# Stick-breaking attention on one Trainium2 core: high parts taken straight from PSUM, weights kept in PSUM for their low part, q stacked by DMA, last key block 128 wide

## The chip, the cores and the metric

The kernel runs on one core of one Trainium2 chip. The metric is the device time of one execution in microseconds (us); smaller is better. The engines are called as the profile calls them: PE (matmul), DVE (VectorE), ACT (ScalarE), POOL (GpSimd) and SP (SyncE, which here only issues DMAs).

## What is computed

The reference is a two-layer trunk over 512 positions of width 1024: an RG-LRU layer, a SwiGLU feed-forward layer (FFN), a stick-breaking attention layer with 16 heads of width 64, and a second FFN, each with an RMSNorm ahead of it and a residual add behind. The change touches the attention alone, whose core is, for each head (cut from the reference):

```python
z = jnp.einsum("bhqd,bhkd->bhqk", qb, k32) * scale
mask = key_pos[None, :] < q_pos[:, None]
log_beta = jax.nn.log_sigmoid(z)
log_1m = jnp.where(mask, jax.nn.log_sigmoid(-z), 0.0)
suffix = lax.cumsum(log_1m, axis=3, reverse=True) - log_1m
wts = jnp.where(mask, jnp.exp(log_beta + suffix), 0.0)
return jnp.einsum("bhqk,bhkd->bhqd", wts, v32)
```

All of it is to be exact to nearly float32.

## The kernel before, in words

**Two parts for every operand.** TensorE multiplies in float32r, a rounded float32. The kernel therefore splits each operand into a high part (a copy into a float32r tile, which rounds) and a low part (the operand minus the high part) and adds the products high by high, high by low and low by high in PSUM. Most of the work of DVE, ACT and POOL is such splitting: weights arrive by DMA as 128x1024 chunks `raw`, ACT copies the high part `wh` (L236) and DVE or POOL subtracts the low part `wl` (L237).

**Attention, per head.** Scores are held transposed, keys on the partitions and queries along the free axis, in four key blocks of 128 keys. Key block `kt` only meets queries from its own block on, so its tile is `ZW[kt]` = 512, 384, 256, 256 queries wide; the last one holds 128 columns more than it needs, which are masked. A head has three PSUM banks: one for block 0, one for block 1, and one for blocks 2 and 3 side by side. Two sets of three banks alternate between even and odd heads, so head h+2 reuses the banks of head h; the last two banks serve the projections and the output. The steps are:

- `proj(t, part)` (PE, L270 to L272): one 128-row tile of q (t even) or k (t odd) for a pair of heads, 24 matmuls of 512 columns in two halves of 12, called P0 and P1 here. `proj_evac1` (DVE, L854) scales it into `tt`. `proj_evac2` splits it: for q into `qh` and `ql` of each head, 64 rows that are written twice, into both halves of the partitions (ACT L863 and L867, DVE L868 and L869), for k into `ks` of each head, high part in one half of the partitions, low part in the other (ACT L874, DVE L875).
- `s1(h)` (PE, L888 to L894): scores of head h, four blocks, each with `qh`, `ql` and a bf16 mask matmul.
- `chain_a(h)`: for each of three banks ACT does Abs, Exp and Ln (L910 to L912), DVE adds max(z, 0) in a `scalar_tensor_tensor` that reads the bank (L913, into `sp`), DVE casts the high part `sph` (L914) and POOL subtracts the low part `spl` (L915). For the third bank DVE also adds its two halves, casts the high part `r` and POOL subtracts the low part (L919 to L921).
- `s2(h)` (PE, L940): 16 matmuls add the suffix sums onto the scores in the same banks.
- `chain_b(h)`: for each bank ACT takes Exp from PSUM into an SBUF tile `t` (L955), DVE casts the high part `awh` (L956); then the low part `awl` is subtracted (L961), on DVE for the second bank (and the third from head 12 on), on POOL for the others.
- `s3(h)` (PE, L970): 8 matmuls, weights times `v`; then ACT copies half of the result (L978) and DVE adds it to the other half into `o` (L979). `osplit` (ACT L996, DVE L997) later splits a pair's `o` for the output projection `out_part`.

**What sets the order.** The loop over h from 0 to 16 is written out under a manual schedule: PE, ACT, DVE and POOL execute in the order of the code, each on its own, and wait on semaphores for one another. The body of iteration h is: P0 of tile t = h+3, `s1(h+1)`, `chain_a(h+1)` of the first two banks, P1 and `proj_evac1`, `chain_a(h+1)` of the third bank, `s3(h-1)`, `proj_evac2(t)`, perhaps an `osplit`, `s2(h)`, `chain_b(h)`. The split of the weights of the next tile is put ahead of `chain_a` on its engines. Only SP's order is left to the scheduler. An iteration with t odd is called a k iteration here (h even), one with t even a q iteration. Tiles of 128x512 come from a ring of reused slots (`new`, `rel`), temporaries from a ring of six (`tmp`); whoever writes a reused slot waits for its last readers.

Of the kernel before, what the change touches and what calls it, by code (L numbers as in the profile page):

```python
# [97 lines left out]
class Kern:  # L98
# [682 lines left out]
    def attention(self):  # L781
        nc, tc = self.nc, self.tc
        mm = nc.tensor.matmul
        ZW = (512, 384, 256, 256)
        QO = (0, 128, 256, 256)
        with ExitStack() as cx:
# [10 lines left out]
            msk = ap_.tile([P, 2 * P], BF16, name="msk")  # L797
# [7 lines left out]
            nc.gpsimd.affine_select(out=msk[:, P:2 * P], in_=msk[:, P:2 * P], compare_op=ALU.is_ge, fill=0.0,  # L805
# [50 lines left out]
            def proj_evac2(t):  # L856
                p, isk = divmod(t, 2)
                tt = self.tt
                lo, hi = slice(0, 64), slice(64, 128)
                if not isk:  # L860
                    for j, (own, oth) in enumerate(((lo, hi), (hi, lo))):
                        qh, ql = self.new("qh", F32R), self.new("ql", F32R)
                        nc.scalar.copy(qh[own], tt[own])  # L863
# [4 lines left out]
                        nc.vector.tensor_tensor(ql[own], tt[own], qh[own].bitcast(F32), ALU.subtract)  # L868
                        nc.vector.tensor_copy(ql[oth], ql[own].bitcast(F32))  # L869
                        heads[2 * p + j] = dict(qh=qh, ql=ql)  # L870
                else:
                    for j, (own, oth) in enumerate(((lo, hi), (hi, lo))):
                        ks = self.new("ks", F32R)
                        nc.scalar.copy(ks[own], tt[own])  # L874
                        nc.vector.tensor_tensor(ks[oth], tt[own], ks[own].bitcast(F32), ALU.subtract)  # L875
                        heads[2 * p + j]["ks"] = ks

            def zslot(h):
                b = zb[3 * (h % 2):3 * (h % 2) + 3]
                return (b[0][:, 0:512], b[1][:, 0:384], b[2][:, 0:256], b[2][:, 256:512]), b  # L880

            def s1(h):
                hd = heads[h]
                zt, b = zslot(h)
                for kt in range(4):
                    qs = slice(QO[kt], S)
                    lk = hd["ks"][:, ts(kt)]
                    mm(zt[kt], lhsT=lk, rhs=hd["qh"][:, qs], start=kt < 3, stop=False, skip_group_check=True)  # L888
                    mm(zt[kt], lhsT=lk, rhs=hd["ql"][:, qs], start=False, stop=False, skip_group_check=True)
                    if kt < 3:  # L890
                        mm(zt[kt][:, 0:P], lhsT=idb, rhs=msk[:, P:2 * P], start=False, stop=True,
                           skip_group_check=True)
                    else:
                        mm(zt[kt], lhsT=idb, rhs=msk, start=False, stop=True, skip_group_check=True)  # L894
                self.rel(hd["qh"], hd["ql"], hd["ks"])

            BW = (512, 384, 512)

            def chain_a(h, banks=(0, 1, 2)):
# [4 lines left out]
                for i in banks:  # L904
                    w = BW[i]
                    e, sp = self.tmp(), self.tmp()
                    sh = sph[i] = self.new("sph", F32R)
                    sl = spl[i] = self.new("spl", F32R)
                    z = b[i][:, :w]
                    nc.scalar.activation(e[:, :w], z, AF.Abs)  # L910
                    nc.scalar.activation(e[:, :w], e[:, :w], AF.Exp, scale=-1.0)
                    nc.scalar.activation(e[:, :w], e[:, :w], AF.Ln, bias=1.0)  # L912
                    nc.vector.scalar_tensor_tensor(sp[:, :w], z, 0.0, e[:, :w], ALU.max, ALU.add)  # L913
                    nc.vector.tensor_copy(sh[:, :w], sp[:, :w])  # L914
                    nc.gpsimd.tensor_tensor(sl[:, :w], sp[:, :w], sh[:, :w].bitcast(F32), ALU.subtract)  # L915
                    if i == 2:
# [28 lines left out]
            def chain_b(h):  # L945
# [3 lines left out]
                ts_ = []  # L949
                for i in range(3):  # L950
                    w = BW[i]
                    t = self.tmp()
                    ts_.append(t)
# [1 line left out]
                    nc.scalar.activation(t[:, :w], b[i][:, :w], AF.Exp)  # L955
                    nc.vector.tensor_copy(wh[:, :w], t[:, :w])  # L956
                for i in range(3):
                    w = BW[i]
# [1 line left out]
                    eng = nc.vector if i == 1 or (i == 2 and h >= 12) else nc.gpsimd  # L960
                    eng.tensor_tensor(wl[:, :w], ts_[i][:, :w], hd["wh"][i][:, :w].bitcast(F32), ALU.subtract)  # L961
# [188 lines left out]
```

## Time and profile before

| what | value |
|---|---|
| runs of the kernel | 1194.64 us median of 3 (1192.91 to 1197.56) |
| the profiled execution | 1194.11 us, its span 1192.4 us |
| PE busy over the span | 1139.0 us (96%) |
| DVE busy over the span | 884.0 us (74%) |
| ACT busy over the span | 647.1 us (54%) |
| POOL busy over the span | 356.8 us (30%) |
| the head loop's s1 and s2, first to last | about 572 to 787 us of the span |

A time inside the profile is counted from the start of the span. Busy time counts an instruction from start to end; two matmuls overlap at their ends, so the distance from start to start is what one costs in a row of them. A row of a timeline gives start, length, engine, line, operation, output and inputs, shape and count; in a table of groups the count is followed by total busy time, mean length in ns, and the idle time of the engine just before, with whoever ended it.

### The profile page before, as it was taken

What the parts mean: (1) busy time and instruction counts of PE and PEld (TensorE: products, weight loads), DVE (VectorE), ACT (ScalarE), POOL (GpSimd) and SP (SyncE); (2) the same over time, 40 slices, a digit from 0 to 9 for tenths busy, and PEclk for the clock granted to TensorE, in tenths of its full rate; (3) what the DMA queues carried; (4) which work ended last, traced back from release to release, by engine and by line L of the source; (5) the groups of instructions that cost most, each with busy time, mean ns of one, the idle gap of its engine ahead of it and who ended that gap; (6) DMA issues with size and microseconds to landing.
All of it is one profiled execution on the core that took longest, in us unless ns stands there. A gap on an engine that the chain in (4) does not pass through costs nothing.

```text
span 1192.4 us, 14205 instructions
## 1 busy us (share of the span) xinstructions
PE 1139.0 (96%) x5363; PEld 939.9 (79%) x5363; DVE 884.0 (74%) x1117; ACT 647.1 (54%) x935; POOL 356.8 (30%) x214
## 2 busy tenths in 40 slices
PE   9999999999999999999989888899999999999995
PEld 6887787888888888888767767678788888888884
DVE  7878889675757656544899999978967666675655
ACT  6698576534343434434677777757553434353431
POOL 2451223111111021451466665632311120211231
PEclk9999999999999999999999999899999999999997
DMA  7222344332323222322111111123422232322201
GB/s 235 85 88 88 107 139 144 106 105 73 121 74 115 80 88 73 104 89 71 53 36 53 37 36 36 36 70 126 154 92 93 84 107 88 124 88 89 71 18 71
DMA packets 30741, 105.83 MB, mean 89 GB/s; under 512 B 3536, under 2 KB 4560, under 8 KB 30672
## 3 DMA queue, kind: packets, MB, share of 16 engines
q1 hardware_dynamic: 30384, 104.40, 26.1%
q8 instruction: 42, 0.69, 0.2%
q10 hardware_dynamic: 288, 0.52, 0.1%
q14 instruction: 27, 0.22, 0.1%
HBM read 102.81 MB, written 2.10 MB: 88 GB/s over the span
## 4 chain that ended last, share of the span: by engine, by line
PE 63%; DVE 20%; ACT 4%; issue 4%; DMA 1%; POOL 1%; DVEq 0%; ACTq 0%; POOLq 0%
PE bank L631 10%; PE bank L632 10%; PE bank L633 10%; PE bank L654 7%; PE bank L652 7%; PE bank L653 7%; DVE wl L237 4%; PE bank L270 3%; PE bank L271 3%; PE bank L272 3%; DVE sph L914 3%; DVE t L913 2%; PE bank L638 1%; DVE r L920 1%; ACT wh L236 1%
## 5 line engine op out<-in xcount | busy, mean ns | idle before, releaser
L237 POOL TENSOR_TENSOR wl<-raw,wh 128x1024 fp32r<-128x1024 f32 (+1 forms) x74 | 178.8, 2416 | 619.6 <-ACT wh L236 619.6
L236 ACT CAST wh<-raw 128x1024 fp32r<-128x1024 f32 (+1 forms) x154 | 156.0, 1016 | 186.4 <-PE bank L633 88.4
L631 PE MATMUL bank<-wh,ow 128*128 128x512 f32 (+1 forms) x480 | 180.2, 375 | 3.8 <-DVE st L389 3.8
L632 PE MATMUL bank<-wl,ow 128*128 128x512 f32 (+1 forms) x480 | 178.9, 373 | 0.0
L633 PE MATMUL bank<-wh,ow 128*128 128x512 f32 (+1 forms) x480 | 178.8, 373 | 0.0
L237 DVE TENSOR_TENSOR wl<-raw,wh 128x1024 fp32r<-128x1024 f32 (+1 forms) x80 | 104.4, 1308 | 45.4 <-ACT wh L236 44.4
L236 ACT CAST wh<-tt 128x1024 fp32r<-128x1024 f32 x66 | 69.4, 1052 | 111.0 <-PE bank L653 55.1
L652 PE MATMUL bank<-hh,wh 128*128 128x512 f32 (+1 forms) x324 | 125.4, 387 | 0.0
L653 PE MATMUL bank<-hl,wh 128*128 128x512 f32 (+1 forms) x324 | 125.3, 387 | 0.0
L654 PE MATMUL bank<-hh,wl 128*128 128x512 f32 (+1 forms) x324 | 125.3, 387 | 0.0
L657 DVE TENSOR_TENSOR x<-x,bank 128x512 f32<-128x512 f32 x87 | 59.6, 685 | 85.2 <-PE bank L654 84.3
L270 PE MATMUL bank<-uh,wh 128*128 128x512 f32 x256 | 105.1, 410 | 4.4 <-DVE t L854 4.1
L237 DVE TENSOR_TENSOR wl<-tt,wh 128x1024 fp32r<-128x1024 f32 x66 | 80.7, 1223 | 36.4 <-ACT wh L236 36.0
L631 PEld LDWEIGHTS bank<-wh,ow 128*128 128x128 f32 x480 | 90.8, 189 | 20.0 <-issue 2.6
L633 PEld LDWEIGHTS bank<-wh,ow 128*128 128x128 f32 x480 | 90.8, 189 | 15.9
L632 PEld LDWEIGHTS bank<-wl,ow 128*128 128x128 f32 x480 | 90.9, 189 | 15.3
L272 PE MATMUL bank<-uh,wl 128*128 128x512 f32 x256 | 101.5, 397 | 1.0 <-DVE wl L237 1.0
L271 PE MATMUL bank<-ul,wh 128*128 128x512 f32 x256 | 102.1, 399 | 0.0
L237 DVE TENSOR_TENSOR wl<-b,wh 128x1024 fp32r<-128x1024 f32 x44 | 54.9, 1247 | 51.7 <-ACT wh L236 51.5
L236 ACT CAST wh<-b 128x1024 fp32r<-128x1024 f32 x44 | 46.3, 1053 | 62.1 <-PE bank L633 26.7
L915 POOL TENSOR_TENSOR spl<-t,sph 128x512 fp32r<-128x512 f32 (+1 forms) x48 | 58.9, 1233 | 58.3 <-DVE sph L914 47.9
L654 PEld LDWEIGHTS bank<-hh,wl 128*128 128x128 f32 x324 | 60.9, 188 | 12.4
(222 smaller groups left out, 2554.6 us busy)
## 6 DMA issues: line engine op xcount, KB each, us to landing
raw<-w_gu SPq DMA_DIRECT2D x44, 512.0 KB, 3.5
b<-w_gu SPq DMA_DIRECT2D x44, 512.0 KB, 4.2
raw<-w_dn SPq DMA_DIRECT2D x44, 512.0 KB, 3.5
raw<-w_qk SPq DMA_DIRECT2D x16, 512.0 KB, 3.5
raw<-w_in SPq DMA_DIRECT2D x14, 512.0 KB, 4.0
raw<-w_ao SPq DMA_DIRECT2D x8, 512.0 KB, 3.6
raw<-w_v SPq DMA_DIRECT2D x8, 512.0 KB, 3.4
raw<-w_bo SPq DMA_DIRECT2D x8, 512.0 KB, 3.5
```

The source lines that it names most:

```text
L236: self.nc.scalar.copy(wh[:, c], raw[:, c])
L237: self.wl_engine(i).tensor_tensor(wl[:, c], raw[:, c], wh[:, c].bitcast(F32), ALU.subtract)
L270: mm(out, lhsT=wh, rhs=xh, start=first, stop=False)
L271: mm(out, lhsT=wh, rhs=xl, start=False, stop=False)
L272: mm(out, lhsT=wl, rhs=xh, start=False, stop=last)
L631: mm(out[j][:, :w], lhsT=oh[:, ts(j)], rhs=wh[:, ws], start=st, stop=False, skip_group_check=True)
L632: mm(out[j][:, :w], lhsT=oh[:, ts(j)], rhs=wl[:, ws], start=False, stop=False, skip_group_check=True)
L633: mm(out[j][:, :w], lhsT=ol[:, ts(j)], rhs=wh[:, ws], start=False, stop=en, skip_group_check=True)
L652: mm(out, lhsT=w[0][:, ws], rhs=h[:, cs], start=st, stop=False, skip_group_check=True)
L653: mm(out, lhsT=w[0][:, ws], rhs=lw[:, cs], start=False, stop=False, skip_group_check=True)
L654: mm(out, lhsT=w[1][:, ws], rhs=h[:, cs], start=False, stop=en, skip_group_check=True)
L657: nc.vector.tensor_tensor(self.x[m], self.x[m], bank, ALU.add)
```

## The change

The attention function is edited in six places; everything else of the kernel is the same.

1. The last key block becomes 128 queries wide (`ZW`, `QO`). Its scores lie in columns 128 to 256 of the third bank (`ZO`), next to block 2 in 256 to 512, so the third bank's ACT and DVE work is 384 wide instead of 512. Its `sp` is one fixed tile `sp2` whose first 128 columns are zeroed once, so that the two halves can still be added. The mask is 128 wide everywhere.
2. `chain_a`: `sph` is no longer a cast of `sp` but a second `scalar_tensor_tensor` that reads the bank again and rounds on its output.
3. The low part of `r` is subtracted by DVE instead of POOL.
4. `chain_b`: ACT takes Exp twice, once from the bank into `awh` (which rounds), once in place in the bank; DVE then subtracts `awh` from the bank into `awl`, for all three banks. The three casts, and POOL's and DVE's subtractions from SBUF, are gone.
5. q: one ACT copy and one DVE subtraction of the whole 128x512 tile make `xh` and `xl` of the pair; eight DMAs of 64x512 on SP's queue copy them into `qh` and `ql` of the two heads.
6. The slots of `xh` and `xl` are given back at once, so the next tiles that take them wait for these DMAs.

```diff
-        ZW = (512, 384, 256, 256)
-        QO = (0, 128, 256, 256)
+        ZW = (512, 384, 256, 128)
+        QO = (0, 128, 256, 384)
+        ZO = (0, 0, 256, 128)
...
-            msk = ap_.tile([P, 2 * P], BF16, name="msk")
+            msk = ap_.tile([P, P], BF16, name="msk")
+            sp2 = [ap_.tile([P, S], F32, name="sp2")]
+            for t in sp2:
+                nc.vector.memset(t[:, 0:P], 0.0)
...
-                    for j, (own, oth) in enumerate(((lo, hi), (hi, lo))):
+                    xh, xl = self.new("qx", F32R), self.new("qy", F32R)
+                    nc.scalar.copy(xh, tt)
+                    nc.vector.tensor_tensor(xl, tt, xh.bitcast(F32), ALU.subtract)
+                    for j, own in enumerate((lo, hi)):
                         qh, ql = self.new("qh", F32R), self.new("ql", F32R)
-                        nc.scalar.copy(qh[own], tt[own])
-                        if t < 3:
-                            nc.vector.tensor_copy(qh[oth], tt[own])
-                        else:
-                            nc.scalar.copy(qh[oth], tt[own])
-                        nc.vector.tensor_tensor(ql[own], tt[own], qh[own].bitcast(F32), ALU.subtract)
-                        nc.vector.tensor_copy(ql[oth], ql[own].bitcast(F32))
+                        for dst, src in ((qh, xh), (ql, xl)):
+                            for part in (lo, hi):
+                                nc.sync.dma_start(dst[part].bitcast(F32), src[own].bitcast(F32))
                         heads[2 * p + j] = dict(qh=qh, ql=ql)
+                    self.rel(xh, xl)
...
-            BW = (512, 384, 512)
+            BR = (slice(0, 512), slice(0, 384), slice(128, 512))
...
-                    e, sp = self.tmp(), self.tmp()
+                    e, sp = self.tmp(), sp2[0] if i == 2 else self.tmp()
...
-                    nc.vector.tensor_copy(sh[:, :w], sp[:, :w])
-                    nc.gpsimd.tensor_tensor(sl[:, :w], sp[:, :w], sh[:, :w].bitcast(F32), ALU.subtract)
+                    nc.vector.scalar_tensor_tensor(sh[:, w], z, 0.0, e[:, w], ALU.max, ALU.add)
+                    nc.gpsimd.tensor_tensor(sl[:, w], sp[:, w], sh[:, w].bitcast(F32), ALU.subtract)
...
-                        nc.gpsimd.tensor_tensor(r[:, HS:], rt[:, :HS], r[:, :HS].bitcast(F32), ALU.subtract)
+                        nc.vector.tensor_tensor(r[:, HS:], rt[:, :HS], r[:, :HS].bitcast(F32), ALU.subtract)
...
                 for i in range(3):
-                    w = BW[i]
-                    t = self.tmp()
-                    ts_.append(t)
+                    w = BR[i]
                     wh = hd["wh"][i] = self.new("awh", F32R)
-                    nc.scalar.activation(t[:, :w], b[i][:, :w], AF.Exp)
-                    nc.vector.tensor_copy(wh[:, :w], t[:, :w])
-                for i in range(3):
-                    w = BW[i]
                     wl = hd["wl"][i] = self.new("awl", F32R)
-                    eng = nc.vector if i == 1 or (i == 2 and h >= 12) else nc.gpsimd
-                    eng.tensor_tensor(wl[:, :w], ts_[i][:, :w], hd["wh"][i][:, :w].bitcast(F32), ALU.subtract)
+                    nc.scalar.activation(wh[:, w], b[i][:, w], AF.Exp)
+                    nc.scalar.activation(b[i][:, w], b[i][:, w], AF.Exp)
+                    nc.vector.tensor_tensor(wl[:, w], b[i][:, w], wh[:, w].bitcast(F32), ALU.subtract)
```

The lines of the changed kernel differ by a few from those of before: its `xh` copy is L866, `xl` L867, the q DMAs L872, `o` L973, the two Exps L953 and L954, and the subtraction of `awl` L955.

The first place is DVE in the q iteration h = 5, from the `o` of head 4 to the first work of the next iteration. In the kernel before there stand there (tile numbers tell the slots apart; `t` are temporaries):

```order
L979 TENSOR_TENSOR o_5278<-bank_76,t_5279 64x512
L868 TENSOR_TENSOR ql_5283<-t_5253,qh_5282 64x512
L869 CAST ql_5283<-ql_5283 64x512
L868 TENSOR_TENSOR ql_5289<-t_5253,qh_5288 64x512
L869 CAST ql_5289<-ql_5289 64x512
L956 CAST awh_5311<-t_5310 128x512
L956 CAST awh_5315<-t_5314 128x384
L956 CAST awh_5319<-t_5318 128x512
L961 TENSOR_TENSOR awl_5324<-t_5314,awh_5315 128x384
L913 SCALAR_TENSOR_TENSOR t_5359<-bank_73,t_5358 128x512
L914 CAST sph_5360<-t_5359 128x512
```

In the changed kernel, from the third bank of `chain_a` on:

```order
L913 SCALAR_TENSOR_TENSOR sp_4059<-bank_72,t_5252 128x384
L914 SCALAR_TENSOR_TENSOR sph_5253<-bank_72,t_5252 128x384
L919 TENSOR_TENSOR t_5261<-sp_4059 128x256
L920 CAST r_507_5262<-t_5261 128x256
L921 TENSOR_TENSOR r_507_5262<-t_5261,r_507_5262 128x256
L973 TENSOR_TENSOR o_5274<-bank_76,t_5275 64x512
L867 TENSOR_TENSOR qy_5279<-t_5250,qx_5278 128x512
L955 TENSOR_TENSOR awl_5311<-bank_73,awh_5310 128x512
L955 TENSOR_TENSOR awl_5316<-bank_74,awh_5315 128x384
L955 TENSOR_TENSOR awl_5321<-bank_75,awh_5320 128x384
L913 SCALAR_TENSOR_TENSOR t_5356<-bank_73,t_5355 128x512
L914 SCALAR_TENSOR_TENSOR sph_5357<-bank_73,t_5355 128x512
```

Four q instructions became one, the three casts are gone, and the three subtractions that now read the banks of head 5 stand behind the whole `chain_a` of head 6, behind `r`, `o` and `xl`; the next `s1` on these banks waits for them.

The second place is ACT in the same iteration, from the copy of L978 (now L972) to the next weight split. Before:

```order
L978 COPY t_5279<-bank_76 64x512
L863 CAST qh_5282<-t_5253 64x512
L867 CAST qh_5282<-t_5253 64x512
L863 CAST qh_5288<-t_5253 64x512
L867 CAST qh_5288<-t_5253 64x512
L955 ACTIVATE t_5310<-bank_73 128x512
L955 ACTIVATE t_5314<-bank_74 128x384
L955 ACTIVATE t_5318<-bank_75 128x512
L236 CAST wh_5328<-raw_4928 128x1024
```

In the changed kernel:

```order
L972 COPY t_5275<-bank_76 64x512
L866 CAST qx_5278<-t_5250 128x512
L953 ACTIVATE awh_5310<-bank_73 128x512
L954 ACTIVATE bank_73<-bank_73 128x512
L953 ACTIVATE awh_5315<-bank_74 128x384
L954 ACTIVATE bank_74<-bank_74 128x384
L953 ACTIVATE awh_5320<-bank_75 128x384
L954 ACTIVATE bank_75<-bank_75 128x384
L236 CAST wh_5325<-raw_4929 128x1024
```

Three q copies went, three Exps came, bank by bank in pairs.

The third place is SP's queue around the q DMAs of one pair in the changed kernel (`raw` are weight loads from DRAM; a count stands where two copies go to the two halves of one tile):

```order
L221 DMA raw_4929<-w_qk 128x1024
L221 DMA raw_5066<-w_qk 128x1024
L872 DMA qh_5019<-qx_5015 64x512 x2
L872 DMA ql_5020<-qy_5016 64x512 x2
L872 DMA qh_5025<-qx_5015 64x512 x2
L872 DMA ql_5026<-qy_5016 64x512 x2
L221 DMA raw_5192<-w_qk 128x1024
L221 DMA raw_5329<-w_qk 128x1024
```

Before, only the weight loads stood there; now eight copies stand between every second pair of them.

More of the change, by code (lines that the diff above doesn't have):

```diff
@@ L804, in attention @@
             nc.gpsimd.memset(msk, NEG)
-            nc.gpsimd.affine_select(out=msk[:, P:2 * P], in_=msk[:, P:2 * P], compare_op=ALU.is_ge, fill=0.0,
+            nc.gpsimd.affine_select(out=msk, in_=msk, compare_op=ALU.is_ge, fill=0.0,
                                     base=0, pattern=[[-1, P]], channel_multiplier=1)
@@ L879, in zslot @@
                 b = zb[3 * (h % 2):3 * (h % 2) + 3]
-                return (b[0][:, 0:512], b[1][:, 0:384], b[2][:, 0:256], b[2][:, 256:512]), b
+                return tuple(b[min(k, 2)][:, ZO[k]:ZO[k] + ZW[k]] for k in range(4)), b
             def s1(h):
@@ L889, in s1 @@
                     mm(zt[kt], lhsT=lk, rhs=hd["ql"][:, qs], start=False, stop=False, skip_group_check=True)
[L890 to L894, printed above, removed]
+                    mm(zt[kt][:, 0:P], lhsT=idb, rhs=msk, start=False, stop=True, skip_group_check=True)
                 self.rel(hd["qh"], hd["ql"], hd["ks"])
-            BW = (512, 384, 512)
+            BR = (slice(0, 512), slice(0, 384), slice(128, 512))
             def chain_a(h, banks=(0, 1, 2)):
@@ L904, in chain_a @@
                 for i in banks:
-                    w = BW[i]
-                    e, sp = self.tmp(), self.tmp()
+                    w = BR[i]
+                    e, sp = self.tmp(), sp2[0] if i == 2 else self.tmp()
                     sh = sph[i] = self.new("sph", F32R)
                     sl = spl[i] = self.new("spl", F32R)
[L909 to L915, printed above, removed]
+                    z = b[i][:, w]
+                    nc.scalar.activation(e[:, w], z, AF.Abs)
+                    nc.scalar.activation(e[:, w], e[:, w], AF.Exp, scale=-1.0)
+                    nc.scalar.activation(e[:, w], e[:, w], AF.Ln, bias=1.0)
+                    nc.vector.scalar_tensor_tensor(sp[:, w], z, 0.0, e[:, w], ALU.max, ALU.add)
+                    nc.vector.scalar_tensor_tensor(sh[:, w], z, 0.0, e[:, w], ALU.max, ALU.add)
+                    nc.gpsimd.tensor_tensor(sl[:, w], sp[:, w], sh[:, w].bitcast(F32), ALU.subtract)
                     if i == 2:
@@ L926, in spt @@
                     return hd["sph"][kt], hd["spl"][kt], 0
-                return hd["sph"][2], hd["spl"][2], 256 * (kt - 2)
+                return hd["sph"][2], hd["spl"][2], ZO[kt]
             def s2(h):
@@ L948, in chain_b @@
                 hd["wh"], hd["wl"] = [None] * 3, [None] * 3
[L949 removed]
                 for i in range(3):
[L951 to L953 removed]
+                    w = BR[i]
                     wh = hd["wh"][i] = self.new("awh", F32R)
[L955 to L958 removed]
                     wl = hd["wl"][i] = self.new("awl", F32R)
[L960 to L961 removed]
+                    nc.scalar.activation(wh[:, w], b[i][:, w], AF.Exp)
+                    nc.scalar.activation(b[i][:, w], b[i][:, w], AF.Exp)
+                    nc.vector.tensor_tensor(wl[:, w], b[i][:, w], wh[:, w].bitcast(F32), ALU.subtract)
             def s3(h):
@@ L967, in s3 @@
                     for kt in range(4):
-                        i, off = (kt, 0) if kt < 2 else (2, 256 * (kt - 2))
+                        i, off = min(kt, 2), ZO[kt]
                         w = ZW[kt]
```

## The prediction

> **What bounds the kernel now.** I read the page first, then the head loop by windows, then the timeline of PE, and the groups of DVE in the loop. The page gives the span; a window from the second to the thirteenth `s2` gives busy times (stretch and length, then PE, weight loads, DVE, ACT, POOL with counts, granted clock, DMA share, GB/s).
>
> ```profile
> span 1192.4 us, 14205 instructions
> ...
> 598.86:748.91 150.05, 131.75 (x662) 105.90 (x661) 147.25 (x202) 114.02 (x194) 92.88 (x72) 0.95 0.12 39
> ```
>
> DVE is busy 147.25 of 150.05 us: in this loop it sets the time, though it is only third on the whole page's account. PE is not full there. The timeline of PE shows where `s2` of heads 0, 1, 12 and 15 begins, and one iteration (h = 4 to 5) in which PE runs without a gap.
>
> ```profile
> 583.69 0.39 PE L940 MATMUL bank<-sph,tri 128*128 128x512 f32 x1
> 598.86 0.40 PE L940 MATMUL bank<-sph,tri 128*128 128x512 f32 x1
> ...
> 653.91 0.81 PE L970 MATMUL bank<-awh,vs 128*128 128x512 f32 x4
> 655.21 0.40 PE L940 MATMUL bank<-sph,tri 128*128 128x512 f32 x1
> 657.45 0.28 PE L940 MATMUL bank<-spl,tri 128*128 128x256 f32 x1
> 657.57 0.40 PE L270 MATMUL bank<-uh,wh 128*128 128x512 f32 x1
> 660.31 0.39 PE L888 MATMUL bank<-qh,ks 128*128 128x512 f32 x1
> 662.00 0.47 PE L270 MATMUL bank<-uh,wh 128*128 128x512 f32 x1
> 664.85 0.80 PE L970 MATMUL bank<-awh,vs 128*128 128x512 f32 x4
> ...
> 748.91 0.40 PE L940 MATMUL bank<-sph,tri 128*128 128x512 f32 x1
> 784.24 0.40 PE L940 MATMUL bank<-sph,tri 128*128 128x512 f32 x1
> ```
>
> From 598.86 to 748.91 there are 11 periods of 13.64 us. PE's own work is the distance 653.91 to 664.85: 10.94 us (`s3` 1.30, `s2` 2.36, P0 2.74, `s1` 1.69, P1 2.85). So up to 2.7 us per head lie open if DVE lets go. Why DVE is full, its groups show (585 to 780 us; the row of L642 is that of the whole execution):
>
> ```profile
> L956 DVE CAST awh<-t 128x512 fp32r<-128x512 f32 x30 | 29.3, 977 | 0.3
> L914 DVE CAST sph<-t 128x384 fp32r<-128x384 f32 x15 | 22.2, 1477 | 0.5
> L914 DVE CAST sph<-t 128x512 fp32r<-128x512 f32 x30 | 20.5, 682 | 1.0
> L913 DVE SCALAR_TENSOR_TENSOR t<-bank,t 128x512 f32<-128x512 f32 x30 | 20.3, 676 | 0.0
> L920 DVE CAST r<-t 128x256 fp32r<-128x256 f32 x15 | 18.9, 1262 | 0.5
> L237 DVE TENSOR_TENSOR wl<-raw,wh 128x1024 fp32r<-128x1024 f32 x7 | 15.0, 2148 | 0.0
> L875 DVE TENSOR_TENSOR ks<-t,ks 64x512 fp32r<-64x512 f32 x14 | 10.4, 745 | 0.3
> L979 DVE TENSOR_TENSOR o<-bank,t 64x512 f32<-64x512 f32 x14 | 9.5, 679 | 0.2
> L868 DVE TENSOR_TENSOR ql<-t,qh 64x512 fp32r<-64x512 f32 x12 | 9.4, 781 | 0.2
> L913 DVE SCALAR_TENSOR_TENSOR t<-bank,t 128x384 f32<-128x384 f32 x15 | 8.2, 547 | 0.0
> L869 DVE CAST ql<-ql 64x512 fp32r<-64x512 f32 x13 | 7.6, 582 | 0.4
> L919 DVE TENSOR_TENSOR t<-t 128x256 f32<-128x256 f32 x15 | 6.2, 415 | 0.0
> L956 DVE CAST awh<-t 128x384 fp32r<-128x384 f32 x15 | 5.3, 353 | 0.0
> L997 DVE TENSOR_TENSOR ol<-o,oh 128x512 fp32r<-128x512 f32 x6 | 4.2, 692 | 0.2
> ...
> L642 DVE TENSOR_TENSOR hl<-bank,hh 128x512 fp32r<-128x512 f32 x40 | 25.6, 682 | 0.0
> ```
>
> A cast of 128x384 takes 0.353 us in L956 and 1.477 in L914, and one of 128x256 takes 1.262 in L920: casts stand still while POOL works. The timelines of DVE and POOL show one that ends just as a POOL instruction does:
>
> ```profile
> 666.72 1.98 DVE L914 CAST sph<-t 128x384 fp32r<-128x384 f32 x1
> ...
> 665.90 2.58 POOL L237 TENSOR_TENSOR wl<-raw,wh 128x1024 fp32r<-128x1024 f32 x1
> ```
>
> Instructions that read PSUM (L913, L979) keep their length.
>
> **DVE, per head.** Removed: casts L956 2 x 0.977 + 0.353 = 2.31, casts L914 2 x 0.682 + 1.477 = 2.84, one `awl` subtraction of 384 columns (L961, as L913's row) 0.55, of q per pair 2 x 0.781 + 2 x 0.582 = 2.73, so 1.36 per head, and the third bank's 128 columns 0.13: 7.19 us. Added: a second L913, 0.676 + 2 x 0.547 = 1.77; three subtractions from PSUM, 0.682 (L642, the very operation) + 2 x 0.547 = 1.78; the low part of `r`, 0.415 (L919's shape); `xl`, 0.692 per pair (L997's shape), 0.35: 4.31. Net 2.88 less: DVE falls from 13.39 (147.25 / 11) to 10.5 us per head, below PE.
>
> With casts at the unblocked 0.353, and for 512 columns an estimate of 0.45 from it, the same ledger removes only about 4.3 and DVE gains nothing. [...] I go by the rows as they stand in the loop.
>
> **ACT, per head.** The timeline of ACT has one `chain_a`: 1.83 us for a 512 bank, 1.50 for a 384 bank, start to start; the Exp groups follow.
>
> ```profile
> 564.66 1.26 ACT L863 CAST qh<-t 64x512 fp32r<-64x512 f32 x2 [3.16 <-DVE t L854]
> ...
> 572.62 0.60 ACT L910 ACTIVATE t<-bank 128x512 f32<-128x512 f32 x1 [0.18 <-PE bank L891]
> ...
> 574.45 0.47 ACT L910 ACTIVATE t<-bank 128x384 f32<-128x384 f32 x1
> ...
> 575.95 0.58 ACT L910 ACTIVATE t<-bank 128x512 f32<-128x512 f32 x1
> ...
> L955 ACT ACTIVATE t<-bank 128x512 f32<-128x512 f32 x30 | 18.0, 600 | 3.2 <-POOL spl L915 2.8
> L955 ACT ACTIVATE t<-bank 128x384 f32<-128x384 f32 x15 | 7.3, 487 | 0.2
> ```
>
> Added: three Exps, 0.600 + 2 x 0.487 = 1.57. Removed: 0.33 in `chain_a`, 0.11 in the first Exps, and per pair four q copies of 0.63 less the one `xh`, 0.95 per head. ACT goes from 10.37 (114.02 / 11) to about 10.6. It does not bind, but nothing is left over: PE 10.94, ACT 10.6, DVE 10.5.
>
> **The new wait.** `s1(h+2)` overwrites the banks of head h. Before, it waited for ACT's Exp; now for DVE's subtraction of that bank, which on DVE stands behind the whole `chain_a(h+1)`, `r`, `o`, the k or q split and an `osplit`. Behind a waiting `s1` stand P1, `s3` and `s2` on PE, and ACT's `chain_a` waits for its scores. This closes a loop of one period, from `s1(h+1)` to `s1(h+2)`:
>
> ```profile
> 571.90 0.39 PE L888 MATMUL bank<-qh,ks 128*128 128x512 f32 x1
> ```
>
> From 571.90 to ACT's first Abs at 572.62, 0.72; `chain_a` on ACT 1.83 + 2 x 1.50 = 4.83; then on DVE two L913 of the third bank 1.09, the sum 0.415, the cast 1.26 (still behind POOL's third `spl`), the low part 0.415, `o` 0.68, two `ks` 1.49 or one `xl` 0.69, `ol` 0.69 in five of the eleven, and the first subtraction 0.68. A k iteration takes 11.59, with `ol` 12.28; a q iteration 10.79, so PE's 10.94, with `ol` 11.48. Over h = 1 to 11: 3 x 12.28 + 2 x 11.59 + 2 x 11.48 + 4 x 10.94 = 126.7 us against 150.05, a gain of 23.3. ACT gets to the same point earlier: 0.72 + 4.83, then the copy of L978, two `ks` and `oh` at about 0.6 each and two Exps 1.2, some 9.2 us, where DVE's first subtraction begins at 10.9 or later. So only DVE counts.
>
> The first period, 583.69 to 598.86, is 15.17: at most 4.2 to gain over 10.94; I take 3. The last three, 748.91 to 784.24, are 35.33: 12.28 for h = 12, 10.10 and 10.79 without a k or q split, gain 2.2.
>
> **Narrow matmuls.** Eight float32r matmuls per head go from 256 to 128 columns. One of 256 costs 0.12 (657.45 to 657.57). The only 128-wide float32 products in the timeline, eight records for four matmuls:
>
> ```profile
> 539.45 1.06 PE L406 MATMUL bank<-t,ones 128*128 128x128 f32 x8
> ```
>
> About 0.11 a record, 0.22 a matmul. So each saves 0.01 or costs up to 0.10; I take none, since the former is one record as here.
>
> **The q DMAs.** A weight load of 512 KB has this row on the page, and its issue this one among the `raw` instructions:
>
> ```profile
> raw<-w_qk SPq DMA_DIRECT2D x16, 512.0 KB, 3.5
> ...
> L221 SPq DMA_DIRECT2D raw<-w_qk x8: 327/328/328, 545.9 to 615.3; - x8
> ```
>
> Eight copies hold SP for 2.6 us per pair, ahead of weight loads that are issued several tiles early: hidden. Head 0 needs its four after about 566.1 (564.66 plus copy and subtraction); two more issues and 3.5 make 570.3, before 571.90. Two iterations later the slack is far larger. But new tiles (`sph`, `awh`, `ks`) take the slots of `xh` and `xl`: DVE's second L913 of the next head comes 3.9 us after `xl` at the earliest (0.68 + 0.72 + 1.83 + 0.68), four issues and 3.5 make 4.8, and `chain_a` and `proj_evac1` are queued behind it. Between 0 and 0.9 per pair; I take 0.3, for five pairs 1.5. [...]
>
> The zeroing of `sp2` (128 columns, once) and the narrower mask lie beside other work.
>
> **Sum.** 23.3 + 3 + 2.2 - 1.5 = 27.0 us. The profiled execution took 1194.11 (its span and 1.7 around it), 0.5 below the median of the runs; 1194.1 - 27.0 = 1167.1.
>
> **Rivals.** (1) PE's floor alone, if the loop through DVE is looser than its means add up to: 11 x 2.70, 4.2 for the first period and 35.33 - 3 x 10.94 = 2.5 for the last three, with 1.1 for the narrow matmuls at 0.11: 37.5, 1156.6. For it: neighbours in DVE's timeline overlap a little. Against it: no hand-over between engines is in my means. (2) The 128-wide matmuls take 0.22: PE needs 11.74, the eight periods below that rise by 4.0 and the first by 0.8: 1171.9. (3) DVE stays blocked where both operands come from SBUF. L237 kept at 2.148 begins after the last subtraction, 1.1 behind the first, and ends 3.25 after `s1` begins, where `chain_a`'s first bank is due at 2.55: 0.7 in five k iterations. The low part of `r` at L237's 2.1 ns per column takes 0.54 instead of 0.415, 0.12 in each period: 4.9 in all, 1172.0. For it: POOL still does `spl`. Against it: POOL loses both `awl`, which ran at the time of L237. (2) and (3) together with 0.3 a period for hand-overs, 4.2: 1181. (4) The change does nothing for the time: by the unblocked ledger DVE's work stays as it was, 1194. Against it stand the blocked rows. (5) Slower: the copies of q run one after another at 3.5 each, 28.0 per pair against 27.3 now, 4 in the loop, and head 0 has its q at 565.3 + 14 = 579.3 instead of 571.90, 7.4 more: 1205.5. It decides from about 3.4 us a copy. Against it: the DMA engines are busy 0.12 of the time in the loop, and nothing in SP's order makes a copy wait for the one just before it.
>
> **Chances.** Forecast 0.62, (1) 0.08, (2) 0.10, (3) 0.10, (4) 0.05, (5) 0.05. What a measurement can tell from no change is 0.5%, 6 us: faster 0.90, same 0.05, slower 0.05. The range runs from (1), 1156.6, to (2) and (3) together, 1181; it leaves out (4) and (5).
>
> **What would show it.** Right: DVE under 85% busy in the loop, no cast but `r` blocked, k iterations longer than q iterations, PE's waits ahead of `s1` put down to DVE's `awl`, periods of 11 to 12.3. Wrong: 128-wide rows of PE 0.2 apart; waits of DVE, ACT or PE on the q DMAs; DVE still full; a period over 12.5.

## The result, and the profile after

The changed kernel takes 1175.82 us (median of 4 runs, 1173.81 to 1177.23) against 1194.10 for the kernel before: a ratio of 0.984, 95% interval 0.982 to 0.987, so 1.6% less time. The profiled execution took 1176.21, 17.9 less than the one before, where 27.0 less was forecast. It is faster, as forecast, and 9 us short.

First the span and the window from the second to the thirteenth `s2`, in the columns used before, and the first `s2`, the second, the thirteenth and the last in PE's timeline, with a stretch of 128-wide matmuls.

```profile
span 1174.5 us, 14328 instructions
```

```profile
596.07:733.92 137.85, 125.58 (x662) 103.18 (x662) 107.34 (x184) 112.79 (x214) 52.45 (x41) 0.96 0.34 92
```

```profile
584.00 0.39 PE L940 MATMUL bank<-sph,tri 128*128 128x512 f32 x1
...
596.07 0.45 PE L940 MATMUL bank<-sph,tri 128*128 128x512 f32 x1
...
680.43 0.27 PE L940 MATMUL bank<-spl,one_n 128*128 128x128 f32 x1
680.54 0.27 PE L940 MATMUL bank<-sph,tri 128*128 128x128 f32 x1
680.65 0.28 PE L940 MATMUL bank<-spl,tri 128*128 128x128 f32 x1
680.76 0.44 PE L270 MATMUL bank<-uh,wh 128*128 128x512 f32 x1
...
733.92 0.45 PE L940 MATMUL bank<-sph,tri 128*128 128x512 f32 x1
...
768.79 0.45 PE L940 MATMUL bank<-sph,tri 128*128 128x512 f32 x1
```

DVE, which had 147.25 of 150.05 us, now has 107.34 of 137.85. Stretch by stretch (us), with the experiment `hold_qx` told below beside it:

| stretch | before | forecast | after | hold_qx |
|---|---|---|---|---|
| start to first `s2` | 583.69 | 583.69 | 584.00 | 583.36 |
| first period | 15.17 | 12.17 | 12.07 | 12.06 |
| eleven periods | 150.05 | 126.7 + 1.5 | 137.85 | 129.35 |
| the rest of the span | 443.49 | 441.3 | 440.58 | 438.83 |

All of the shortfall lies in the eleven periods: 12.2 us gained for 21.8. The waits from 585 to 780 us say where to look (engine, line, what it waited for, total, times, longest).

```profile
PE bank L892 <- DVE awl L955: 16.2, 10, 4.1
PE bank L270 <- DVE awl L955: 4.7, 1, 4.7
DVE ol L991 <- DMA qh<-qx: 4.5, 1, 4.5
DVE sph L914 <- DMA ql<-qy: 2.5, 2, 1.4
```

PE waits ahead of `s1` (L892) for `awl`, as forecast; the single wait of 4.7 at L270 is a matmul of `out_part`, told below. But DVE waits 7 us for the q copies, where 1.5 was set down. DVE's timeline has the longest wait, and SP's (issue time, two issues to a row) its cause.

```profile
696.59 0.67 DVE L867 TENSOR_TENSOR qy<-t,qx 128x512 fp32r<-128x512 f32 x1
701.72 0.69 DVE L991 TENSOR_TENSOR ol<-o,oh 128x512 fp32r<-128x512 f32 x1 [4.46 <-DMA qh<-qx]
702.33 1.61 DVE L955 TENSOR_TENSOR awl<-bank,awh 128x512 fp32r<-128x512 f32 x3
```

```profile
695.06 1.11 SPq L872 DMA_DIRECT2D qh<-qx  x2
697.33 1.10 SPq L872 DMA_DIRECT2D ql<-qy  x2
698.48 1.24 SPq L872 DMA_DIRECT2D qh<-qx  x2
699.77 1.24 SPq L872 DMA_DIRECT2D ql<-qy  x2
```

`ol` was given the slot of `xh`. The last readers of `xh`, the second head's two copies, stand in SP's queue behind the first head's two from `xl`, which wait for `xl` at 697.26; at 0.55 to 0.62 us an issue they are out at 699.72 and landed 2 us later. Behind `ol` stands the subtraction that `s1` at 703.07 needs. Windows from one `s1` to the next (columns as above) show the two periods around it, and the same two in `hold_qx`, where no instruction waits for a q copy:

```profile
686.25:703.07 16.82, 12.72 (x61) 10.37 (x61) 10.22 (x18) 9.97 (x19) 5.67 (x4) 0.84 0.40 100
703.07:716.89 13.82, 13.29 (x60) 10.69 (x61) 9.87 (x18) 9.07 (x18) 3.33 (x3) 0.83 0.09 32
```

```profile
684.12:695.64 11.52, 11.12 (x61) 9.10 (x61) 10.13 (x18) 9.98 (x19) 3.43 (x4) 1.00 0.24 71
695.64:707.74 12.10, 11.12 (x60) 9.10 (x60) 9.81 (x18) 9.08 (x18) 5.64 (x4) 1.00 0.42 108
```

The first period is 5.30 longer: 1.60 in PE's busy time and 3.70 in its waits. The second is 1.72 longer though nothing waits for a copy there: PE is busy 13.29 in place of 11.12 for the same 60 matmuls, at a granted clock of 0.83 in place of 1.00. Here the stalls of PE were paid a second time, as a lower clock behind them; the last section shows that this is not always so.

### The profile page after: what moved, and what is told of

The parts are those of the page before. It is cut to its first block, busy times and chain, and to the rows that moved or that the text cites. A ratio compares the mean times of both kernels' runs of the same rounds, so it can differ in the third digit from the quotient of the medians.

```text
span 1174.5 us, 14328 instructions
## 1 busy us (share of the span) xinstructions
PE 1127.7 (96%) x5363; PEld 934.9 (80%) x5363; DVE 823.5 (70%) x1086; ACT 645.2 (55%) x963; POOL 298.5 (25%) x170
## 4 chain that ended last, share of the span: by engine, by line
PE 67%; DVE 13%; ACT 6%; issue 3%; DMA 2%; SPq 0%; POOL 0%; DVEq 0%; ACTq 0%; POOLq 0%
PE bank L631 10%; PE bank L632 10%; PE bank L633 10%; PE bank L654 7%; PE bank L652 7%; PE bank L653 7%; PE bank L270 4%; PE bank L271 4%; PE bank L272 4%; DVE wl L237 4%; PE bank L638 1%; DVE tt L76 1%; ACT wh L236 1%; PE bank L940 1%; PE bank L892 1%
## 5 line engine op out<-in xcount | busy, mean ns | idle before, releaser
L237 POOL TENSOR_TENSOR wl<-raw,wh 128x1024 fp32r<-128x1024 f32 (+1 forms) x74 | 177.7, 2401 | 639.6 <-ACT wh L236 637.0
L237 DVE TENSOR_TENSOR wl<-raw,wh 128x1024 fp32r<-128x1024 f32 (+1 forms) x80 | 97.4, 1220 | 46.2 <-ACT wh L236 45.3
L270 PE MATMUL bank<-uh,wh 128*128 128x512 f32 x256 | 103.8, 406 | 1.5 <-ACT uh L325 0.9
L237 DVE TENSOR_TENSOR wl<-tt,wh 128x1024 fp32r<-128x1024 f32 x66 | 80.6, 1222 | 34.8 <-ACT wh L236 34.5
L237 DVE TENSOR_TENSOR wl<-b,wh 128x1024 fp32r<-128x1024 f32 x44 | 54.8, 1246 | 51.8 <-ACT wh L236 51.6
L652 PEld LDWEIGHTS bank<-hh,wh 128*128 128x128 f32 x324 | 60.9, 188 | 12.1
```

Of the source, the lines that this page charges most:

```text
L237: self.wl_engine(i).tensor_tensor(wl[:, c], raw[:, c], wh[:, c].bitcast(F32), ALU.subtract)
L270: mm(out, lhsT=wh, rhs=xh, start=first, stop=False)
L652: mm(out, lhsT=w[0][:, ws], rhs=h[:, cs], start=st, stop=False, skip_group_check=True)
```

## The experiments

**Theory A**: the period is set by the order of DVE's work ahead of the `awl` subtraction, as in the prediction's loop, and what was missed is the slot wait and the clock after it. **Theory B**: PE, ACT or the clock would set the period anyway. Further rivals stand with the runs. Ratios are to the kernel before on the same chip; two kernels are compared by the difference of their ratios, times 1194.1; the "give or take" is the two intervals' half widths, added in squares. First four kernels on the slots and DVE's order.

**hold_qx**

```
-                    self.rel(xh, xl)          # in proj_evac2
+                    self.qxy = xh, xl
...
                         chain_b(h)
+                    if t < 16 and t % 2 == 0:
+                        self.rel(*self.qxy)   # behind osplit and chain_b
```

> The changed kernel with one difference: the buffers of xh and xl (qx, qy) are given back at the end of the iteration, behind chain_b and osplit, so that no ol and no sph stands in them at once. Theory A (the order of DVE sets the period, and a wait of DVE ahead of the awl subtraction counts in full): the 4.5 us of ol and the 2.5 of sph behind the q DMAs go, the period of 16.8 falls to 12 to 13, and the time by 4.5 to 7, to 1169 to 1171. Theory B (PE, ACT and the clock after each stall would have set the time anyway): within 2 us of the changed kernel, 1174 to 1178. Rival C (two buffers fewer for the length of an iteration make other tiles wait): slower than 1178, with waits of DVE or ACT ahead of sph, awh or ks on PE.

Measured: 1165.93, ratio 0.9771 (0.9754 to 0.9788), against 0.9841 (0.9816 to 0.9867): 8.4 less than the changed kernel, give or take 3.7. B and C fall; A's 4.5 to 7 is within that, on its low side. In the profiles the eleven periods are 8.5 shorter, 129.35, and the single ones are those of the prediction's sums: PE's timeline has `s1` of heads 5, 6 and 7 in it, a k iteration of 11.39 (11.59 summed) and a q iteration of 10.97 (10.94). The first and the last row are `s1` of heads 2 and 13, the ends of the eleven loops that the prediction summed.

```profile
592.36 0.50 PE L892 MATMUL bank<-qh,ks 128*128 128x512 f32 x1 [1.05 <-DVE awl L955]
...
626.50 0.39 PE L892 MATMUL bank<-qh,ks 128*128 128x512 f32 x1
...
637.89 0.50 PE L892 MATMUL bank<-qh,ks 128*128 128x512 f32 x1 [0.40 <-DVE awl L955]
...
648.86 0.39 PE L892 MATMUL bank<-qh,ks 128*128 128x512 f32 x1
...
718.95 0.50 PE L892 MATMUL bank<-qh,ks 128*128 128x512 f32 x1
```

With `ol`, k iterations take 11.99 to 12.11 (12.28 summed) and the q iteration shown above 11.52 (11.48).

**late_ol**

```
+                    if h < NH:
+                        s2(h)
+                        chain_b(h)
                     if 6 <= h < 14 and 2 * nsp + 1 < h:
                         osplit(nsp)
                         nsp += 1
-                    if h < NH:
-                        s2(h)
-                        chain_b(h)
```

> The changed kernel with osplit emitted behind s2(h) and chain_b(h), so that ol stands on DVE behind the three awl subtractions instead of ahead of them. Theory A: ahead of s1 DVE loses 0.69 in each of six iterations (h = 6 to 10 and 12), and of the 4.5 us wait only what is left after the three subtractions, some 2.5, which falls into DVE's slack: 4 to 8 us less, 1168 to 1172, and the periods of h = 6 to 12 come near those of h = 1 to 5 (10.5 to 11.5). Theory B: the long periods of the second half are the clock's or PE's own; within 2 us of the changed kernel, 1174 to 1178.

Measured: 1166.13, ratio 0.9765 (0.9748 to 0.9781), 9.1 less than the changed kernel, give or take 3.6: A again, a little over its price, and not B. The wait of `ol` is gone, 3.3 us of `sph` on copies from `xl` remain, and the eleven periods take 128.50. Both edits take away the stall of `ol`, so their gains should overlap in part; no run has these two alone together (`hold_late_ks` has both and a third edit, and gains 17.0).

**q_order**

```
+                    for n, src in (("qh", xh), ("ql", xl)):
+                        for j, own in enumerate((lo, hi)):
+                            for part in (lo, hi):
+                                nc.sync.dma_start(heads[2 * p + j][n][part].bitcast(F32), src[own].bitcast(F32))
```

> The changed kernel with the eight q copies of a pair issued in another order, the four from xh first and then the four from xl; nothing is given back later. Theory A (SP issues them one after another at 0.55 to 0.62, and the second head's two from xh stood behind the first head's two from xl): the last reader of xh is issued 2.4 us earlier, so the 4.46 us wait of ol falls to about 2.1; the waits of sph on the copies from xl stay at 2.5 in all. 2.4 less, and up to 3.8 more if the granted clock then stays at 1.00 in the two windows in which it was 0.84 and 0.83: 1169 to 1173.5. Rival G (what counts is how long the copies take to land, whatever the order): the wait stays over 4, 1174 to 1178.

Measured: 1172.50, ratio 0.9816 (0.9801 to 0.9831): in A's range, but 3.0 less than the changed kernel, give or take 3.5, is not settled by the time alone. The wait settles it: it fell from 4.46 to 1.72, so the order of issue made most of it, and G falls. SP's timeline has the copies of that pair (four issues to a row):

```profile
691.86 2.40 SPq L873 DMA_DIRECT2D qh<-qx  x4
694.60 2.39 SPq L873 DMA_DIRECT2D ql<-qy  x4
```

The last one from `xl` is out 2.45 us after `xl` (694.54), where it was 3.75 (701.01 after 697.26); so `sph` no longer waits at all, which A had not foreseen. That the gain is no larger has a reason in the timelines of DVE and POOL:

```profile
696.26 2.71 DVE L991 TENSOR_TENSOR ol<-o,oh 128x512 fp32r<-128x512 f32 x1 [1.72 <-DMA qh<-qx]
698.89 1.61 DVE L955 TENSOR_TENSOR awl<-bank,awh 128x512 fp32r<-128x512 f32 x3
```

```profile
696.09 2.34 POOL L237 TENSOR_TENSOR wl<-raw,wh 128x1024 fp32r<-128x1024 f32 x1 [3.35 <-ACT wh L236]
```

`ol`, with both operands in SBUF, takes 2.71 in place of 0.69 and ends only after POOL's `wl` does, at 698.43. So what the shorter wait won was in good part lost again.

**hold_late_ks**: `hold_qx` and `late_ol`, and of a k tile

```
-                        proj_evac2(t)
+                        proj_evac2(t, (0,) if t % 2 else (0, 1))
...
                         chain_b(h)
+                    if t < 16 and t % 2:
+                        proj_evac2(t, (1,))
```

> hold_qx and late_ol together, and of a k tile the second head's split also behind chain_b (that head is needed one iteration later). Theory A: ahead of the first awl subtraction DVE has 0.69 less in every k iteration and no osplit and no DMA wait: the k iteration's loop falls from 11.6 to 10.9, where PE's own 10.94 takes over; against the changed kernel 8 to 14 us less, 1162 to 1168, with PE's waits ahead of s1 nearly gone. Theory B: no lower than the better of the two alone by over 2 us, with PE waiting for ACT's scores in place of awl.

Measured: 1158.29, ratio 0.9699 (0.9682 to 0.9716), 17.0 less than the changed kernel, give or take 3.7: A, at or over the upper end of its 8 to 14. This is the fastest version found and beats both kernels. Its window of the eleven periods:

```profile
594.76:717.71 122.95, 120.37 (x662) 100.53 (x661) 111.43 (x185) 112.41 (x214) 52.90 (x41) 1.00 0.39 103
```

PE is busy 120.37 of 122.95 at full granted clock: 11 times the 10.94 that the prediction read off as its floor is 120.3. B does hold from here on:

**r_add**

```
-                        nc.vector.tensor_copy(r[:, :HS], rt[:, :HS])
+                        nc.vector.tensor_tensor(r[:, :HS], sp[:, :HS], sp[:, HS:], ALU.add)
```

> hold_late_ks with the high part of r made by a second addition with float32r output (0.42) instead of the cast (0.99). Theory A: 0.57 less on the path to awl and to s2, in every period; the loop of 122.95 has 2.6 left above PE's floor of 120.3 and the first and last periods some 2: 0 to 4 us below hold_late_ks, 1154 to 1158. Theory B: no effect, 1158, as PE is the bound already.

Measured: 1159.71, ratio 0.9711 (0.9693 to 0.9728), not to be told from `hold_late_ks`, so B, with A's lower end not excluded: DVE's path hardly counts any more.

The other kernels price the parts of the change. Four undo one on `hold_qx` (or, for q, on the changed kernel), two do one alone on the kernel before. No run prices part 3, the low part of `r` on DVE, by itself.

**undo_q**: `proj_evac2` makes `qh` and `ql` as before.

> The changed kernel with the q split of before (four ACT copies, two subtractions and two casts per pair on DVE, no DMAs); all else as changed. Theory A: in a q iteration DVE carries 2.73 in place of 0.69 ahead of awl, 12.8 instead of 10.94 in h = 1, 3, 5, 11 and 13.5 instead of 11.5 in h = 7 and 9, 11.6 us, less the 7 us of DMA slot waits: 3 to 6 slower than the changed kernel, 1179 to 1182. Rival C (the q rework is the main gain): 11 to 14 slower, 1187 to 1190. Rival D (the DMAs cost more than they give): faster than the changed kernel, 1166 to 1173.

Measured: 1178.39, ratio 0.9872 (0.9854 to 0.9889), just under A's range, 3.7 slower than the changed kernel, give or take 3.7. Its first period is 16.36, but its eleven periods take 136.84, 1.0 less than the changed kernel's. Beside `hold_qx`, also without slot waits and on the same chip, it is 12.5 slower (1178.39 against 1165.93). So the q split is worth some 12 us when no slot waits are in its way, and the change as made lost about two thirds of that in its slots (8.4 of 12.5, with the 3.7 of each comparison still open). C and D both fall.

**undo_b**

```
-                    nc.scalar.activation(wh[:, w], b[i][:, w], AF.Exp)
-                    nc.scalar.activation(b[i][:, w], b[i][:, w], AF.Exp)
-                    nc.vector.tensor_tensor(wl[:, w], b[i][:, w], wh[:, w].bitcast(F32), ALU.subtract)
+                    nc.scalar.activation(t[:, w], b[i][:, w], AF.Exp)
+                    nc.vector.tensor_copy(wh[:, w], t[:, w])
...
+                    eng = nc.vector if i == 1 or (i == 2 and h >= 12) else nc.gpsimd
+                    eng.tensor_tensor(wl[:, w], ts_[i][:, w], hd["wh"][i][:, w].bitcast(F32), ALU.subtract)
```

> hold_qx with chain_b as before: Exp to an SBUF tile, a DVE cast for awh, awl subtracted from SBUF, on POOL for the first bank and (up to h = 11) the third. Theory A (casts on DVE stand still while POOL works): DVE loses 1.78 of PSUM subtractions per head and gets 2.3 of casts at 0.98 and 0.35 and 0.55 of one subtraction, and its wl goes back towards 2.1 us; DVE 9.9 + 1.1 + 0.4 = 11.4 per head and nearly full, the awl wait ahead of s1 gone: loop 126 to 131, time within 4 us of hold_qx, 1162 to 1170, 512-wide casts 0.7 to 1.0. Rival E (casts cost their unblocked 0.35 to 0.45): DVE 9.8 per head, no wait on awl, so PE's floor: 1155 to 1160, and this part of the change is a loss.

Measured: 1165.74, ratio 0.9758 (0.9743 to 0.9773): not to be told from `hold_qx` (1.6 less, give or take 2.7), as A has it. The window of the eleven periods and two DVE groups:

```profile
595.88:725.13 129.25, 122.46 (x662) 101.98 (x662) 126.76 (x197) 96.61 (x178) 78.89 (x61) 0.99 0.36 94
```

```profile
L956 DVE CAST awh<-t 128x384 fp32r<-128x384 f32 x32 | 27.2, 888 | 0.4 <-ACT t L955 0.3
...
L956 DVE CAST awh<-t 128x512 fp32r<-128x512 f32 x16 | 6.7, 418 | 0.5 <-ACT t L955 0.4
```

DVE is full again, 126.76 of 129.25. A 384-wide cast takes 0.888 where the unblocked one had 0.353, and the 512-wide one, for which POOL waits, 0.418. The period is the same by another road: a full DVE without the wait on `awl` in place of a slack DVE with it.

**undo_stt**

```
-                    nc.vector.scalar_tensor_tensor(sh[:, w], z, 0.0, e[:, w], ALU.max, ALU.add)
+                    nc.vector.tensor_copy(sh[:, w], sp[:, w])
```

> hold_qx with sph made by a DVE cast of sp again, in place of the second scalar_tensor_tensor from PSUM. Theory A: the casts take 0.68 (512) and 0.6 to 1.5 (384) behind POOL's spl, up to 1.1 more per head, 0.9 of it on the path from the third bank's Ln to awl: loop 9 to 10 longer, the first and last periods 2: 1174 to 1178. Rival E (POOL has half of its work left, so casts run at 0.35 to 0.45): DVE 0.2 to 0.4 less per head, 1161 to 1166.

Measured: 1167.90, ratio 0.9775 (0.9758 to 0.9793). A's price missed. E comes nearest, with a range that ends at 1166, 2 below the run. The run cannot be told from `hold_qx` (0.5 more, give or take 2.9). DVE's casts in it:

```profile
L914 DVE CAST sph<-t 128x384 fp32r<-128x384 f32 x15 | 11.4, 759 | 0.5
L914 DVE CAST sph<-sp 128x384 fp32r<-128x384 f32 x15 | 6.0, 400 | 0.5
L914 DVE CAST sph<-t 128x512 fp32r<-128x512 f32 x14 | 6.0, 427 | 0.5
```

Together 1.59 per head, against 2.84 before and 1.77 for the second `scalar_tensor_tensor`. With `awl` off POOL, only one of the three is still blocked in part (0.759 against 0.400 for the same shape).

**wide_last**

```
-        ZW = (512, 384, 256, 128)
-        QO = (0, 128, 256, 384)
-        ZO = (0, 0, 256, 128)
+        ZW = (512, 384, 256, 256)
+        QO = (0, 128, 256, 256)
+        ZO = (0, 0, 0, 256)
...
-            BR = (slice(0, 512), slice(0, 384), slice(128, 512))
+            BR = (slice(0, 512), slice(0, 384), slice(0, 512))
```

> hold_qx with the fourth block 256 columns wide again, half of it masked, and the third bank 512 wide in chain_a and chain_b. Theory A (the loop through awl): 0.33 more in ACT's chain and 0.13 more for each of one or two DVE instructions ahead of awl, in every period that is above PE's floor, and 0.1 on PE: 5 to 8 slower than hold_qx, 1171 to 1174. Theory B (narrowing only shortens work that something hides): within 2 us of hold_qx, 1164 to 1168. Rival H (128-wide float32r matmuls cost double): faster than hold_qx by 3 or more.

Measured: 1180.75, ratio 0.9879 (0.9863 to 0.9896): 12.9 slower than `hold_qx`, give or take 2.8, well over A's price; B and H fall. The eleven periods take 139.55, 10.2 more. A k iteration goes from 11.39 to 12.38, of which ACT's 0.33 and 0.26 of two wider `scalar_tensor_tensor`s were counted. What was not is the cast of `r`, which stands still while POOL works on the third `spl` (in the changed kernel's trace one such cast runs from 694.62 to 695.61, the `spl` from 694.40 to 695.46). That `spl` and that cast in `wide_last`:

```profile
L919 POOL TENSOR_TENSOR spl<-sp,sph 128x512 fp32r<-128x512 f32 x15 | 20.3, 1353 | 17.7 <-DVE sph L918 14.6 <-PE bank L944 1.1 <-DMA raw<-w_qk 1.0
```

```profile
L924 DVE CAST r<-t 128x256 fp32r<-128x256 f32 x15 | 19.0, 1265 | 0.5
```

And the `spl` in `hold_qx`, then the cast in the changed kernel, with its L237:

```profile
L915 POOL TENSOR_TENSOR spl<-sp,sph 128x384 fp32r<-128x384 f32 x15 | 16.2, 1077 | 8.2 <-DVE sph L914 6.1 <-PE bank L940 1.6 <-ACT qx L866 0.4
```

```profile
L920 DVE CAST r<-t 128x256 fp32r<-128x256 f32 x15 | 14.8, 990 | 0.5
...
L237 DVE TENSOR_TENSOR wl<-raw,wh 128x1024 fp32r<-128x1024 f32 x7 | 8.5, 1217 | 0.8 <-ACT wh L236 0.8
```

The same cast of 256 columns takes 1.265 behind a 512-wide `spl` and 0.990 behind a 384-wide one: 0.28 of the 0.40 us of a k iteration that were not counted. The clock took part as well: over the eleven periods PE is busy 127.69 us at a granted clock of 0.96, where `hold_qx` has 123.35 at 0.99. How much of the 10.2 each of these made is not separated.

**before_b**: the kernel before with the new `chain_b` (whole 512, 384 and 512 columns).

> The kernel before with one part of the change, chain_b: Exp twice, once to awh and once in place in PSUM, and awl on DVE from PSUM. Theory A: DVE falls from 13.4 to 12.3 per head, and the new loop through awl (0.72 + 4.83 + 0.33 on ACT, then on DVE L913, its cast, the sum, r, o, the split and the first awl) takes 12.1 in a k and 13.3 in a q iteration, 0.7 more with ol: loop 142 to 146, time 1184 to 1190. Rival F (this part alone makes the gain, as the casts it removes are the costliest): 12.3 per head throughout, with POOL's relief less, 1172 to 1180. Rival E (unblocked ledger): no gain or a loss, 1194 to 1200.

Measured: 1185.71, ratio 0.9923 (0.9909 to 0.9937), 9.2 less than before, give or take 1.7, as A has it; its eleven periods take 143.0. Its casts of `sph` already fell to 0.427 (512 columns) and 0.700 (384).

**before_q**: the kernel before with the new q split.

> The kernel before with one part of the change, the q split per pair with its DMAs. Theory A (DVE is full before, so what it is spared counts): 1.0 less per head, 11 in the loop and up to 4 in the first period; the slots of xh and xl are used again soon here too, which takes 0 to 10 back: 1179 to 1190. Rival D (the DMAs cost as much as they spare): within 4 us of before, 1190 to 1198.

Measured: 1185.54, ratio 0.9917 (0.9902 to 0.9931), 9.9 less, give or take 1.7, in A's range; here too DVE's `sph` waits 5.5 us in all for copies from `xl`.

## Why the prediction was right, and where it failed

**Direction and mechanism.** DVE bound the loop and was let go: 107.34 / 11 = 9.8 us per head where 10.5 was forecast. The loop through `awl` set the period afterwards, and with the slot waits out of the way its sum holds: from `s1` of head 2 to `s1` of head 13 `hold_qx` takes 718.95 - 592.36 = 126.59 us, where 126.7 was summed. Ten of the eleven loops are within 0.4 of their sums; one, of 12.63 for 11.59, ran at a clock of 0.86 (last section). That the total agrees to 0.1 is luck: the others, mostly shorter than summed, make up for it.

The window between the second and the thirteenth `s2` nevertheless shows 129.35, because it is another stretch. In iteration h = 1 alone, the kernel puts P1 and `proj_evac1` ahead of `s1`, not behind it, so the `s2` at the start of the window follows the `s1` of its iteration by 3.06 us and the one at its end by 5.82. The prediction set a sum of loops from `s1` to `s1` against a window from `s2` to `s2`, and that is 2.65 us of what was missing.

Two agreements owe something to luck. The first period came out as forecast (12.17, measured 12.07), but its gain of 3 was a choice between 0 and 4.2. The rest of the span gave 2.9 for a forecast 2.2, but not from the place that was meant: the last three periods, 733.92 to 768.79, gave 0.46 (34.87 for 35.33), and 2.45 came behind the last `s2`, where the sum has no term. In the last of the three a matmul of `out_part` writes a bank of head 14 and waits for its `awl`, a form of the new wait that the prediction did not list:

```profile
761.14 0.80 PE L270 MATMUL bank<-oh,wh 128*128 128x512 f32 x1 [4.66 <-DVE awl L955]
```

The time lies inside the stated range of 1156.6 to 1181, but by none of the roads from which its ends were built: rival (1) did not happen, and (2) and (3), which made the upper end, both fell. Of the signs that were to show it wrong, two came: DVE waited on the q DMAs, and the mean period was 137.85 / 11 = 12.53, over 12.5.

**The step that failed: the q DMAs, 1.5 us.** It cost 137.85 - 129.35 = 8.5 us in the eleven periods (8.4, give or take 3.7, by the ratios): 7.0 more than was set down, of the 9.65 by which these periods missed the forecast. The other 2.65 is the stretch told above. The 0.3 us per pair was the author's choice between 0 and 0.9, which no run shows; DVE's waits for the copies came to 7.0 us. Four things were wrong in this step. Issues were priced at a weight load's 0.33 and took 0.55 to 0.62. SP's order was written down but not followed: the last reader of `xh` stands behind copies that wait for `xl`. The list of tiles that take the slots (`sph`, `awh`, `ks`) left out `ol`, which comes at once and stands right ahead of `awl`; a wait there enters the loop in full. And each us of it was priced as one us, though PE's clock fell after the stall, to 0.83 in the period shown. The landing time, by contrast, was taken too long: 3.5, where the page has 2.4 for these copies (KB each, then median us from issue to landing).

```profile
qh<-qx SPq DMA_DIRECT2D x32, 128.0 KB, 2.4
```

**The ledger of removed casts.** That casts stand still while POOL works is confirmed by `undo_b`, where those of 384 columns take 0.888 in place of 0.353. But the savings were added up as if each were independent. Once `chain_b` had taken work off POOL (busy 60.30 of 140.00 us in `before_b`, 92.88 of 150.05 before), the casts of `sph` were mostly free already (0.427 and 0.700 there, 0.682 and 1.477 before), and the second `scalar_tensor_tensor`, listed at 2.84 removed against 1.77 added, brought nothing that can be measured. Neither does `chain_b` on `hold_qx`, though alone it brought 9.2: the parts relieve the same engine. The rows of before were right for the kernel before only.

**The narrow block.** The matmuls cost nothing, as taken: 128-wide rows start 0.11 apart. The shorter chain on ACT and DVE was in the loop's sum, but never named as a gain of its own; on `hold_qx` it is as large as the q split's, 12.9 us. The cast of `r` was kept at 1.262 "still behind POOL's third `spl`"; the narrower `spl` brought it to 0.990.

**The rivals.** (1), PE's floor of 1156.6, is not what happened, but `hold_late_ks` reaches it within 2 us once the order is changed. (2) fell by the 0.11. (3) fell: L237 on DVE went from 2.148 to 1.217. (4) fell by the result and by DVE's 107.34. (5) had the copies in series at 3.5 each; what is in series is their issue, at 0.6.

**Open.** Which stall of PE brings the clock down is not settled (below), and so the split of the 8.5 us into waits and clock was made for the two periods shown only.

## What to carry to other kernels

A buffer handed back to a shared pool behind a DMA is a wait for whoever gets it next: look up who that is, what stands behind it on its engine, and in which order the issuing queue comes to the last reader; hold the buffer a little longer, or move the taker behind the work that others wait for. An engine that works in order gives its result at the end of a list: what a loop waits for goes ahead of what nobody needs soon, and here that holding and reordering was worth 17 us, nearly as much as the whole change. Savings on one engine do not add, so a part is priced against the kernel that the other parts leave behind.

## What the runs showed of the hardware

A stall of PE of the same length may or may not cost clock. Here are a period of the changed kernel whose `s1` had waited 2.17 us, and the same period of `hold_qx`, whose `s1` had waited 2.18:

```profile
603.53:615.04 11.51, 11.12 (x61) 9.10 (x61) 9.21 (x17) 10.08 (x20) 5.70 (x4) 1.00 0.46 115
```

```profile
602.90:615.53 12.63, 12.63 (x60) 10.31 (x60) 9.27 (x17) 9.59 (x19) 5.68 (x4) 0.86 0.43 105
```

The second lost 1.1 us at a clock of 0.86; in PE's timeline of `hold_qx` the 512-wide matmuls stand 0.43 apart up to 607.89 and 0.23 apart after that.

```profile
606.61 0.63 PE L271 MATMUL bank<-ul,wh 128*128 128x512 f32 x1
607.04 0.63 PE L272 MATMUL bank<-uh,wl 128*128 128x512 f32 x1
...
608.39 0.40 PE L270 MATMUL bank<-uh,wh 128*128 128x512 f32 x1
608.63 0.40 PE L271 MATMUL bank<-ul,wh 128*128 128x512 f32 x1
```

So the length of a stall alone does not decide whether the clock falls, 1.00 or 0.86 behind 2.17 and 2.18 us; what else does, these runs do not show.

Not only casts are held up by POOL: a subtraction with both operands in SBUF took 2.71 us in place of 0.69 (`q_order`, beside a `wl` of 2.34 on POOL). Subtractions that read PSUM kept their length: three of them take 1.61 us in `q_order` from 698.89 on, with POOL idle, and 1.61 in the changed kernel from 602.80 on, where POOL's `wl` begins at 603.66. And the issue of a 128 KB copy within SBUF held SP for 0.55 to 0.62 us in the rows above (median of the changed kernel 0.59), where a 512 KB weight load (L221) holds it for 0.33 in the median; one weight load of the changed kernel took 0.99, and whether the kind of copy or the queue ahead of it makes the price was not tried.
